# Macaron half steps of a decoder layer: seven products of quarters, with tokens stationary

## The chip, the cores and the metric

The kernel runs on one core of a Trainium2 chip. The metric is the device time of one launch in microseconds (us). Inputs and outputs are fp32; operands of most products are split in two parts of the type fp32r, and three products of parts (high by high, high by low, low by high) stand for one fp32 product.

## The reference

One layer, 512 tokens, model width 1024, hidden width 2816:

```python
h = h + 0.5 * swiglu(rms_norm(h, g_ffn1), w_ffn1_gu, w_ffn1_down)
h = h + hybrid_mixer(rms_norm(h, g_mix), w_in, b_gate, conv_w, w_conv_out, w_attn_out, w_o)
h = h + memory_cross_attention(rms_norm(h, g_cross), rms_norm(mem, g_mem), w_cq, w_ckv, w_co)
h = h + 0.5 * swiglu(rms_norm(h, g_ffn2), w_ffn2_gu, w_ffn2_down)
out = rms_norm(h, g_final)

def swiglu(x, w_gu, w_down):
    gate, up = jnp.split(x @ w_gu, 2, axis=-1)
    return (jax.nn.silu(gate) * up) @ w_down
```

`rms_norm` divides each token by its root mean square and multiplies by a gain per channel. The mixer (a gated convolution and stick-breaking attention of 8 heads) and the cross attention (4 heads over 256 memory tokens) keep their products.

## The kernel before

Activations lie with channels on the partitions and 512 tokens along the rows: h is eight tiles of 128x512. All products outside attention and the value projections are tiles `W^T x`: a block of 128x128 of the weights is stationary and 512 tokens stream past it. `mm3` (L147) issues the three matmuls of a pair of parts.

The work is a list of steps in TensorE's order (`prog`, L154). `run` (L159) goes through the list; weights are loaded by SP two blocks ahead (`load`, 1 MB each into `raw`) and split two steps ahead (`prepare`: ACT copies the high part, DVE subtracts it from the source for the low part, 128x1024 each). Each engine executes its instructions in the order in which the program writes them.

A macaron half step is `ffn` (L324). Up: for 22 chunks of the hidden width a gate tile and an up tile, 24 matmuls of 512 columns each; evacuated on DVE (times 1 / rms, times silu of the gate from ACT) and split into two parts that stay in SBUF. Down: eight output tiles, each 66 matmuls over the 22 chunks, in pairs; `after_ffn1` (L412) adds half of a tile to h as soon as it is summed, splits h for the next stage and squares it for the next norm, while TensorE sums the next tile. `lead` (L378) starts the first two tiles chunk by chunk as x comes in; the norm's factor is applied at evacuation, and evacuations wait (`held`) until it is there. `finish` (L784) does the last two tiles of the second half step by halves of the tokens, so that the first half's norm and output (L814, partly on POOL) run beside the second half's products.

1 / rms (`Norm`): ACT squares, DVE adds, TensorE sums over partitions (`reduce`), DVE does twelve short steps on columns, and a diagonal times a matrix of ones spreads the factor along the rows.

## Time and profile before

| | |
|---|---|
| median of 3 runs | 1440.4 us (1439.62 to 1440.59) |
| span of the profiled execution | 1438.3 us (its own time outside the span is not listed; the median lies 2.1 us above the span) |
| TensorE busy, mean granted clock | 1420.2 us (99%), 0.994 |
| VectorE (DVE), ScalarE (ACT), GpSimd (POOL) busy | 730.0, 543.8, 8.6 us |
| read from and written to memory (HBM) | 135.31 MB, 2.10 MB |

Busy times are of one execution. Matmuls are pipelined: one of 512 columns is listed with 390 ns, and what it costs is the distance from one start to the next. Idle time of an engine costs something only where TensorE, which is busy throughout, waits for it.

### The profile page before, as it was taken

Reading aid. Unit: us, or ns where it says so; the run is one execution under the profiler, and the core shown is the slowest. Engines: PE = TensorE matmul, PEld = TensorE weight load, DVE = VectorE, ACT = ScalarE, POOL = GpSimd, SP = SyncE. Lnnn points to the kernel's source line nnn. Section 1 sums busy time; section 2 is a strip of 40 time slices with the busy share of each in tenths; the row PEclk is TensorE's granted clock in tenths of the full one; section 3 lists DMA queues with packets and bytes.
Section 4 is the critical chain, followed back from the end, with each engine's and each line's share of the span. In section 5 each row is a group of like instructions: output and inputs, shape, how many; then the busy total and the mean of one; then the engine's idle time right before and its main releaser. Section 6 shows DMA issues by size and latency. Waiting matters only on the chain.

```text
span 1438.3 us, 15958 instructions
## 1 busy us (share of the span) xinstructions
PE 1420.2 (99%) x6644; PEld 1193.5 (83%) x6644; DVE 730.0 (51%) x1073; ACT 543.8 (38%) x714; POOL 8.6 (1%) x20
## 2 busy tenths in 40 slices
PE   8999999999999999999999999999999999999996
PEld 7888888888888888888888888988888888888885
DVE  7544444333566664676544447655564544443324
ACT  5323232222365554566332225454442332322222
POOL 0000000000000000000000000000000000000001
PEclk9999999999999999999999999999999999999998
DMA  6223223232312222122223223422223222323221
GB/s 206 88 91 114 88 88 110 81 110 84 114 59 88 85 91 88 62 86 88 88 88 117 89 88 135 147 100 80 97 88 106 99 88 95 111 85 100 88 81 59
DMA packets 23288, 138.43 MB, mean 96 GB/s; under 512 B 2480, under 2 KB 5808, under 8 KB 8880
## 3 DMA queue, kind: packets, MB, share of 16 engines
q1 hardware_dynamic: 23216, 137.42, 28.0%
q8 instruction: 52, 0.85, 0.2%
q14 instruction: 20, 0.16, 0.0%
HBM read 135.31 MB, written 2.10 MB: 96 GB/s over the span
## 4 chain that ended last, share of the span: by engine, by line
PE 98%; DVE 1%; DMA 0%; issue 0%; ACT 0%; SPq 0%; DVEq 0%
PE ps L148 30%; PE ps L150 30%; PE ps L149 30%; PE ps L244 2%; PE ps L246 2%; PE ps L245 2%; PE z L509 1%; PE z L149 1%; PE z L150 1%; PE z L148 1%; DMA h<-in_xt 0%; PE z L277 0%; PE ps L725 0%; PE z L312 0%; DVE a L814 0%
## 5 line engine op out<-in xcount | busy, mean ns | idle before, releaser
L148 PE MATMUL ps<-a,whi 128*128 128x512 f32 (+1 forms) x1878 | 717.9, 382 | 3.0 <-ACT whi L112 3.0
L150 PE MATMUL ps<-a,wlo 128*128 128x512 f32 (+1 forms) x1878 | 717.7, 382 | 0.0
L149 PE MATMUL ps<-a,whi 128*128 128x512 f32 (+1 forms) x1878 | 717.4, 382 | 0.0
L112 ACT ACTIVATE whi<-raw 128x1024 fp32r<-128x1024 f32 (+2 forms) x270 | 269.5, 1002 | 744.6 <-PE ps L149 472.3
L118 DVE TENSOR_TENSOR wlo<-raw,whi 128x1024 fp32r<-128x1024 f32 (+2 forms) x270 | 309.9, 1151 | 212.3 <-ACT whi L112 211.3
L148 PEld LDWEIGHTS ps<-a,whi 128*128 128x128 f32 x1878 | 353.8, 188 | 71.0 <-ACT whi L112 3.7
L149 PEld LDWEIGHTS ps<-a,whi 128*128 128x128 f32 x1878 | 353.7, 188 | 68.1 <-DVE a L120 0.2
L150 PEld LDWEIGHTS ps<-a,wlo 128*128 128x128 f32 x1878 | 353.7, 188 | 68.0
L108 DVE TENSOR_TENSOR a<-ps,a 128x512 f32<-128x512 f32 (+1 forms) x144 | 96.6, 675 | 260.0 <-PE ps L150 259.6
L112 ACT ACTIVATE a<-a 128x512 fp32r<-128x512 f32 (+2 forms) x99 | 58.0, 586 | 83.1 <-DVE a L108 43.4
L118 DVE TENSOR_TENSOR a<-a,a 128x512 fp32r<-128x512 f32 (+2 forms) x99 | 62.2, 632 | 16.4 <-ACT a L112 12.5
L108 DVE TENSOR_TENSOR a<-a,a 128x512 f32<-128x512 f32 x52 | 36.0, 692 | 4.4
L245 PE MATMUL ps<-wlo,a 128*128 128x512 f32 x96 | 37.4, 390 | 0.0
L244 PE MATMUL ps<-whi,a 128*128 128x512 f32 x96 | 37.4, 390 | 0.0
L246 PE MATMUL ps<-whi,a 128*128 128x512 f32 x96 | 37.4, 390 | 0.0
L118 DVE TENSOR_TENSOR w<-w,w 128x1408 fp32r<-128x1408 f32 x16 | 26.0, 1626 | 20.9 <-ACT w L112 20.9
L477 DVE SCALAR_TENSOR_TENSOR w<-z,w 128x512 f32<-128x512 f32 (+1 forms) x24 | 14.7, 641 | 39.9 <-ACT w L474 35.6
L108 DVE TENSOR_TENSOR a<-a,ps 128x512 f32<-128x512 f32 x16 | 11.0, 688 | 45.6 <-PE ps L150 45.6
L260 ACT ACTIVATE a<-h 128x512 f32<-128x512 f32 (+1 forms) x42 | 24.5, 597 | 9.5 <-DVE h L802 9.5
L330 ACT ACTIVATE a<-a 128x512 f32<-128x512 f32 x44 | 27.1, 616 | 2.1 <-DVE a L108 2.1
L268 DVE TENSOR_TENSOR a<-a,a 128x512 f32<-128x512 f32 (+1 forms) x42 | 26.4, 628 | 0.9 <-ACT a L260 0.5
L120 DVE SCALAR_TENSOR_TENSOR a<-h,cst,a 128x512 fp32r<-128x512 f32 x32 | 23.7, 746 | 5.6 <-ACT a L114 5.6
(118 smaller groups left out, 750.3 us busy)
## 6 DMA issues: line engine op xcount, KB each, us to landing
raw<-in_w_gu SPq DMA_DIRECT2D x43, 1024.0 KB, 4.9
raw<-in_w_dn SPq DMA_DIRECT2D x16, 896.0 KB, 4.6
raw<-in_w_dn SPq DMA_DIRECT2D x8, 1024.0 KB, 5.0
raw<-in_w_qk SPq DMA_DIRECT2D x8, 1024.0 KB, 4.9
raw<-in_w_cx SPq DMA_DIRECT2D x8, 1024.0 KB, 4.9
raw<-in_w_gate SPq DMA_DIRECT2D x8, 1024.0 KB, 4.8
raw<-in_w_mix SPq DMA_DIRECT2D x8, 1024.0 KB, 4.9
raw<-in_w_v SPq DMA_DIRECT2D x4, 1024.0 KB, 4.9
```

The source lines that it names most:

```text
L108: nc.vector.tensor_tensor(out=out_, in0=a, in1=b, op=ALU.mult)
L112: nc.scalar.activation(hi, src, AF.Copy)
L118: nc.vector.tensor_tensor(out=lo, in0=src, in1=hi.bitcast(F32), op=ALU.subtract)
L148: nc.tensor.matmul(ps, wh, xh, start=first, stop=False, **kw)
L149: nc.tensor.matmul(ps, wh, xl, start=False, stop=False, **kw)
L150: nc.tensor.matmul(ps, wl, xh, start=False, stop=last, **kw)
L244: nc.tensor.matmul(ps[t], xh[:, c], hi[:, k, :], start=kk == 0, stop=False)
L245: nc.tensor.matmul(ps[t], xh[:, c], lo[:, k, :], start=False, stop=False)
L246: nc.tensor.matmul(ps[t], xl[:, c], hi[:, k, :], start=False, stop=kk == KC - 1)
L260: nc.scalar.activation(sq, h, AF.Square)
L268: nc.vector.tensor_tensor(out=self.acc, in0=self.acc, in1=sq, op=ALU.add)
L330: nc.scalar.activation(g, g, AF.Silu)
```

## The change

Both half steps are computed as products of 2x2 quarters, seven instead of eight, with 15 sums of quarters (Strassen's scheme in Winograd's form), and the roles of the operands are exchanged: 128 tokens by 128 channels are stationary, and 512 (in the last up block 256) columns of weights stream. Results have tokens on the partitions.

Up: x has quarters by tokens (first and last 256) and by channels (chunks 0 to 3 and 4 to 7). `prepare` makes the seven left operands once, with two sums on DVE and two on POOL. A block of weights has 512 gate and 512 up columns as its two column halves, five such blocks and one with 256 and 256. Its four quarters come in units of 128x1024; of each unit POOL makes four sums (`Weights.make`), and all seven right operands are split by ACT and DVE, in 5 buffers of each part, 3 units ahead. `PRODUCTS` gives the order of the seven: A, B, C name the PSUM banks, of which several products add into one. Evacuation joins the banks: silu(gate) times up.

The hidden tiles are turned by TensorE (`turn`, 8 transposes for two chunks), copied by ACT, their four sums made by POOL, and the seven left operands written to DRAM (`hidden`). Down reads them back per product (`part`), splits them, and adds half of each product to the residual, which now has tokens on the partitions (`ht`, for the first half step loaded a second time from x; for the second half step made by 32 transposes, `turn_back`). After the first half step 32 transposes bring h back to channels on partitions. The last norm's factor is now a column per token, and the gain a row. The stages get pools of their own that reuse each other's memory; all 8 PSUM banks are one pool. `lead` and `finish` go.

```diff
+PRODUCTS = ((1, "A"), (5, "C"), (6, "A"), (2, "B"), (7, "A"), (4, "A"), (3, "C"))
+UNITS_AHEAD, LOADS_AHEAD, WBUFS = 3, 4, 5
...
-    def ffn(xs, r, w_gu, w_dn, evac, lead=None, finish=None):
...
+        NEEDS = {1: (0,), 5: (0, 1), 6: (0, 1, 2), 2: (3,), 7: (1, 2), 4: (3,), 3: (2,)}
+        def make(self, i, u):
+            t = self.t
+            b11, b12, b22 = (t.get((q, u)) for q in range(3))
+            def sum_(out, a, b, op=ALU.subtract):
+                nc.gpsimd.tensor_tensor(out=out, in0=a, in1=b, op=op)
+            if i == 5:
+                t["T1", u] = pools["w"].tile([P, 1024], F32, tag="raw", name=nm("raw"))[:, :self.size[u]]
+                sum_(t["T1", u], b12, b11)
+            elif i == 6:
+                sum_(b12, b22, b12)
+                sum_(b11, b12, b11, ALU.add)
+            elif i == 4:
+                sum_(t[3, u], t[3, u], b11)
+            src = {1: b11, 2: t.get((3, u)), 3: b22, 4: t.get((3, u)), 5: t.get(("T1", u)), 6: b11, 7: b12}[i]
+            hi, lo = (pools["w"].tile([P, 1024], F32R, tag=tag, name=nm(tag), bufs=WBUFS) for tag in ("whi", "wlo"))
+            m = self.size[u]
+            split_hi(hi[:, :m], src)
+            split_lo(lo[:, :m], src, hi[:, :m])
+            return [(hi[:, j:j + self.n], lo[:, j:j + self.n]) for j in range(0, m, self.n)]
...
+            def product(place, i, name, units, t):
+                parts = [x for u in units for x in u.parts]
+                if place in (0, 1, 3):
+                    banks[name, t] = bank((P, w.n))
+                ps = banks[name, t]
+                for k, (bh, bl) in enumerate(parts):
+                    ah, al = side(i, k, t)
+                    first, last = k == 0, k == len(parts) - 1
+                    kw = dict(skip_group_check=place not in (0, 1, 3))
+                    nc.tensor.matmul(ps, ah, bh, start=first and place in (0, 1, 3), stop=False, **kw)
+                    nc.tensor.matmul(ps, ah, bl, start=False, stop=False, **kw)
+                    nc.tensor.matmul(ps, al, bh, start=False, stop=last, **kw)
+                evac(i, t, ps)
...
+            for fn, units in self.steps:
+                if units is not None:
+                    upto = min(place[id(units[-1])] + 1 + UNITS_AHEAD, len(self.units))
+                    while made < upto:
+                        x = self.units[made]
+                        need = max(index[id(x.w), q, x.u] for q in Weights.NEEDS[x.i])
+                        load(need + 1 + LOADS_AHEAD)
+                        x.parts = x.w.make(x.i, x.u)
+                        made += 1
+                fn()
...
+    def up(g, r, w_gu, before):
+        plan, parts, sums = Plan(), {}, {}
+        hidden = [dram.tile([P, 7, n, 256], F32, name=nm("hidden")) for _, n in SEGS]
...
+            def put(i, src):
+                hi, lo = (pools["s"].tile([P, 1024], F32R, tag="side", name=nm("s")) for _ in range(2))
+                nc.scalar.activation(half(hi), src, AF.Copy)
+                nc.vector.tensor_tensor(out=half(lo), in0=src, in1=half(hi).bitcast(F32), op=ALU.subtract)
+                parts[i] = hi, lo
...
+            for k in range(KC):
+                nc.scalar.activation(x[k // 4][:, k % 4, :], h[k], AF.Copy, scale=col(g, k))
+                if k == 3:
+                    put(1, a11)
+            s1 = sum_(nc.vector, a21, a22, ALU.add)
+            put(5, s1)
+            s2 = sum_(nc.vector, s1, a11, ALU.subtract)
+            put(6, s2)
+            put(2, a12)
+            put(7, sum_(nc.gpsimd, a11, a21, ALU.subtract))
+            put(4, a22)
+            put(3, sum_(nc.gpsimd, a12, s2, ALU.subtract))
...
+            def fused(out, ps, t):
+                nc.vector.scalar_tensor_tensor(out=out, in0=ps, scalar=rr(t), in1=out, op0=ALU.mult, op1=ALU.add)
+            def evac(i, t, ps):
+                if i == 1:
+                    a["g", t] = small()
+                    nc.scalar.activation(a["g", t], ps, AF.Copy, scale=rr(t))
+                elif i == 6:
+                    a["u", t] = small()
+                    nc.scalar.activation(a["u", t], ps, AF.Copy, scale=rr(t))
+                elif i == 2:
+                    fused(a["g", t], ps, t)
+                    nc.scalar.activation(a["g", t], a["g", t], AF.Silu)
+                elif i == 7:
+                    a["u", t + 2] = small()
+                    nc.scalar.activation(a["u", t + 2], ps, AF.Copy, scale=rr(t + 2))
+                    fused(a["u", t + 2], a["C", t], t + 2)
+                elif i == 5:
+                    a["C", t] = ps
+                elif i == 4:
+                    a["g", t + 2] = small()
+                    nc.scalar.activation(a["g", t + 2], ps, AF.Silu, scale=rr(t + 2))
+                    mul(a["g", t + 2], a["g", t + 2], a.pop(("u", t + 2)))
+                elif i == 3:
+                    fused(a["u", t], ps, t)
+                    mul(a["g", t], a["g", t], a.pop(("u", t)))
...
+        def turn(a, j, m, place):
+            e = pools["e"].tile([P, 8, 256], F32, tag="E", name=nm("e"))
+            for c, (chunk, order) in enumerate(((j, (2, 3, 0, 1)), (j + m, (0, 1, 2, 3)))):
+                ps = bank()
+                for n, t in enumerate(order):
+                    nc.tensor.transpose(out=ps[:, n * P:(n + 1) * P], in_=a["g", t][:, chunk * P:(chunk + 1) * P],
+                                        identity=ident)
+                nc.scalar.activation(e[:, 2 * c:2 * c + 2, :].rearrange("p k c -> p (k c)"), ps, AF.Copy)
+            a21, a11, a12, a22, s1, s2, s3, s4 = (e[:, q, :] for q in range(8))
+            for out_, x, y, op in ((s1, a21, a22, ALU.add), (s2, s1, a11, ALU.subtract),
+                                   (s3, a11, a21, ALU.subtract), (s4, a12, s2, ALU.subtract)):
+                nc.gpsimd.tensor_tensor(out=out_, in0=x, in1=y, op=op)
+            seg = next(n for n, (p, q) in enumerate(SEGS) if p <= place < p + q)
+            nc.sync.dma_start(out=hidden[seg][:, :, place - SEGS[seg][0], :], in_=e[:, 1:, :])
...
+            if late is not None:
+                for slot, job in zip((2, 4), late):
+                    turns[slot] = job
+            if b == 0:
+                plan.step(prepare)
+                plan.step(before)
+            plan.block(w, side, evac, turns)
+            m = n // P // 2
+            late = [lambda a=a, j=j, m=m, p=place + j: turn(a, j, m, p) for j in range(m)]
+            place += m
...
+            def part(i, s=s, n=n, parts=parts):
+                src = pools["s"].tile([P, n * 256], F32, tag="hid", name=nm("hid"), bufs=3)
+                nc.sync.dma_start(out=src, in_=hidden[s][:, SIDE.index(i)].rearrange("p n c -> p (n c)"))
+                hi, lo = (pools["s"].tile([P, n * 256], F32R, tag=tag, name=nm(tag), bufs=3) for tag in ("shi", "slo"))
+                split_hi(hi, src)
+                split_lo(lo, src, hi)
+                parts[i] = hi, lo
...
+                def add(tok, half, src):
+                    o = ht[:, tok, half * 512:(half + 1) * 512]
+                    nc.vector.scalar_tensor_tensor(out=o, in0=src, scalar=0.5, in1=o, op0=ALU.mult, op1=ALU.add)
...
-    def lead(block, evacs):
...
+    def norm1():
+        for k in range(KC):
+            r1.add(h[k])
+        r1.reduce()
+    with phase(w=14):
+        with phase(s=14, e=3, a=11):
+            load_x()
+            hidden = up(G_FFN1, r1, w_gu1, norm1)
+        with phase(t=1, s=3, a=2):
+            ht = pools["t"].tile([P, S // P, D], F32, name="ht1")
+            nc.sync.dma_start(out=ht, in_=xr.rearrange("t p d -> p t d"))
+            sums = spool.tile([P, 4], F32, name="sums1", bufs=1)
+            def squares(i, t):
+                tok = {3: t, 4: t + 2}.get(i)
+                if tok is not None:
+                    sq = pools["a"].tile([P, D], F32, tag="sq", name=nm("sq"))
+                    nc.scalar.activation(sq, ht[:, tok, :], AF.Square, accum_out=sums[:, tok:tok + 1])
+            down(hidden, ht, w_dn1, w_dt1, lambda: None, squares)
+            rm.newton(sums)
+            turned = {}
+            for m in range(KC):
+                ps = bank()
+                for t in range(4):
+                    nc.tensor.transpose(out=ps[:, t * P:(t + 1) * P], in_=ht[:, t, m * P:(m + 1) * P], identity=ident)
+                nc.scalar.activation(h[m], ps, AF.Copy)
+    mixer_pools = phase(w=3, a=61)
+    mixer_pools.__enter__()
...
-    step(rm.reduce)
...
+    rf.reduce()
+    mixer_pools.__exit__(None, None, None)
...
+            def turn_back():
+                for t in range(4):
+                    for half in range(2):
+                        ps = bank()
+                        for m in range(4):
+                            nc.tensor.transpose(out=ps[:, m * P:(m + 1) * P],
+                                                in_=h[4 * half + m][:, t * P:(t + 1) * P], identity=ident)
+                        nc.scalar.activation(ht[:, t, half * 512:(half + 1) * 512], ps, AF.Copy)
...
+            ro.newton(both)
+            for t in (2, 3, 0, 1):
+                o = pools["a"].tile([P, D], F32, tag="o", name=nm("o"))
+                nc.vector.scalar_tensor_tensor(out=o, in0=ht[:, t, :], scalar=ro.cols[:, t:t + 1], in1=gain,
+                                               op0=ALU.mult, op1=ALU.mult)
+                nc.sync.dma_start(out=out[t], in_=o)
```

Three places show the order. First the start, on TensorE. Before (z is the warm-up's bank, ps an output tile, a the parts of x, whi and wlo those of weights):

```order
L81 MATMUL z_76<-ones 128x128 x8
L148 MATMUL ps_105<-a_118,whi_101 128x512
L148 MATMUL ps_106<-a_118,whi_102 128x512
L149 MATMUL ps_105<-a_119,whi_101 128x512
L150 MATMUL ps_105<-a_118,wlo_103 128x512
L149 MATMUL ps_106<-a_119,whi_102 128x512
```

After (s is a left operand's part, a the sum of the squares):

```order
L106 MATMUL z_72<-ones 128x128 x8
L302 MATMUL z_183<-ones,a_160 128x1 x4
L425 MATMUL ps_256<-whi_222,s_120 128x512
L426 MATMUL ps_256<-wlo_223,s_120 128x512
L427 MATMUL ps_256<-whi_222,s_121 128x512
```

The reduction of the first norm (L302) now stands ahead of the first product. It waits for the last of the sums of squares (L293) on DVE, whose queue after the change reads so up to there (L482 makes left operands of x, L143 splits weights):

```order
L293 TENSOR_TENSOR a_160<-a_160,a_171 128x512
L482 TENSOR_TENSOR s_137<-raw_134,s_136 128x1024
L482 TENSOR_TENSOR s_141<-x_115,s_140 128x1024
L482 TENSOR_TENSOR s_147<-raw_144,s_146 128x1024
L293 TENSOR_TENSOR a_160<-a_160,a_174 128x512
L143 TENSOR_TENSOR wlo_223<-raw_212,whi_222 128x1024
L482 TENSOR_TENSOR s_151<-x_115,s_150 128x1024
L482 TENSOR_TENSOR s_157<-raw_154,s_156 128x1024
L293 TENSOR_TENSOR a_160<-a_160,a_177 128x512
L143 TENSOR_TENSOR wlo_229<-raw_214,whi_228 128x1024
L293 TENSOR_TENSOR a_160<-a_160,a_180 128x512
```

The last sum of squares comes behind the left operands of all seven products and two splits of weights; before, the sums of squares stood after the splits of the first two tiles, which TensorE had been fed with.

Second, the middle of up. DVE before (a_367 is 1 / rms along the rows, a others gate, up and their parts):

```order
L118 TENSOR_TENSOR a_803<-a_799,a_802 128x512
L108 TENSOR_TENSOR a_837<-ps_812,a_367 128x512
L118 TENSOR_TENSOR wlo_841<-raw_736,whi_840 128x1024
L108 TENSOR_TENSOR a_869<-ps_844,a_367 128x512
L108 TENSOR_TENSOR a_869<-a_869,a_837 128x512
L118 TENSOR_TENSOR wlo_879<-raw_806,whi_878 128x1024
L118 TENSOR_TENSOR a_873<-a_869,a_872 128x512
L108 TENSOR_TENSOR a_907<-ps_882,a_367 128x512
```

DVE after, in the third block (wlo are low parts of right operands, L517 evacuates):

```order
L143 TENSOR_TENSOR wlo_901<-raw_808,whi_900 128x1024
L143 TENSOR_TENSOR wlo_951<-raw_844,whi_950 128x1024
L143 TENSOR_TENSOR wlo_955<-raw_578,whi_954 128x1024
L143 TENSOR_TENSOR wlo_987<-raw_628,whi_986 128x1024
L143 TENSOR_TENSOR wlo_992<-raw_808,whi_991 128x1024
L517 SCALAR_TENSOR_TENSOR a_873<-ps_995,ny_210,a_873 128x512
L143 TENSOR_TENSOR wlo_1045<-raw_844,whi_1044 128x1024
L517 SCALAR_TENSOR_TENSOR a_888<-ps_1010,ny_210,a_888 128x512
L143 TENSOR_TENSOR wlo_1049<-raw_766,whi_1048 128x1024
L517 SCALAR_TENSOR_TENSOR a_1064<-ps_904,ny_210,a_1064 128x512
```

On POOL there was nothing between the constants and the output:

```order
L87 AFFINE_SELECT fence<-fence 128x128
L89 AFFINE_SELECT fence<-fence 128x256
L100 AFFINE_SELECT a_2621<-ones 128x128
L814 TENSOR_TENSOR a_10238<-a_10098,a_10188 128x256
L814 TENSOR_TENSOR a_10238<-a_10100,a_10188 128x256
```

POOL after, while the third block runs: turned tiles of the second (e) and sums of the fourth's weights (raw):

```order
L557 TENSOR_TENSOR e_930<-e_930 128x256
L385 TENSOR_TENSOR raw_1130<-raw_898,raw_852 128x1024
L557 TENSOR_TENSOR e_930<-e_930 128x256
L385 TENSOR_TENSOR raw_898<-raw_1086,raw_898 128x1024
L557 TENSOR_TENSOR e_930<-e_930 128x256 x2
L385 TENSOR_TENSOR raw_1166<-raw_948,raw_890 128x1024
L385 TENSOR_TENSOR raw_948<-raw_1122,raw_948 128x1024
L557 TENSOR_TENSOR e_1025<-e_1025 128x256 x4
L385 TENSOR_TENSOR raw_852<-raw_898,raw_852 128x1024
L385 TENSOR_TENSOR raw_890<-raw_948,raw_890 128x1024
L385 TENSOR_TENSOR raw_1128<-raw_1128,raw_852 128x1024
L385 TENSOR_TENSOR raw_1164<-raw_1164,raw_890 128x1024
```

DVE has a low part in nearly every row, and POOL has gained sums of 128x1024 whose results a block's later low parts are made of.

Third, from up to down of the first half step, on SP. Before:

```order
L170 DMA raw_1506<-in_w_gu 128x2048
L170 DMA raw_1576<-in_w_gu 128x2048
L170 DMA raw_1646<-in_w_dn 128x2048
L170 DMA raw_1716<-in_w_dn 128x1792
L170 DMA raw_1786<-in_w_dn 128x1792
```

After (ht is the residual, hid a left operand of down, e the last turned chunks; the store from e_2055 waits for POOL):

```order
L559 DMA hidden_113<-e_1864 896x1x256
L559 DMA hidden_113<-e_1949 896x1x256
L371 DMA raw_2198<-in_w_dn 128x1024
L659 DMA ht_2085<-in_xr 128x4x1024
L559 DMA hidden_113<-e_2055 896x1x256
L371 DMA raw_2206<-in_w_dn 128x1024
L598 DMA hid_2088<-hidden_112 128x1536
L598 DMA hid_2184<-hidden_112 128x1536
L598 DMA hid_2254<-hidden_112 128x1536
```

Before, the next blocks of weights were all that SP had to bring; now the first operand of down (hid_2088) stands behind the store of the last turned chunks.

## Rows read from the trace of the kernel before

**Rows 1.** Page: busy us by engine (share, instructions), and the last chain.

```profile
PE 1420.2 (99%) x6644; PEld 1193.5 (83%) x6644; DVE 730.0 (51%) x1073; ACT 543.8 (38%) x714; POOL 8.6 (1%) x20
...
PE 98%; DVE 1%; DMA 0%; issue 0%; ACT 0%; SPq 0%; DVEq 0%
```

**Rows 2.** Windows: stretch, length, busy us by engine, granted clock, DMA share, GB/s.

```profile
6.00:14.00 8.00, 5.77 (x21) 4.22 (x20) 5.12 (x15) 5.68 (x16) 0.00 (x0) 0.87 1.00 345
...
60.00:230.00 170.00, 170.00 (x752) 140.85 (x751) 78.20 (x94) 51.70 (x63) 0.00 (x0) 1.00 0.29 99
230.00:345.00 115.00, 115.00 (x509) 95.29 (x508) 44.02 (x50) 31.94 (x40) 0.00 (x0) 1.00 0.28 93
```

**Rows 3.** Timeline, TensorE at 256 columns: start us, us, engine, line, out<-in, count, idle.

```profile
1416.59 0.28 PE L150 MATMUL ps<-a,wlo 128*128 128x256 f32 x1
...
1416.71 0.28 PE L148 MATMUL ps<-a,whi 128*128 128x256 f32 x1
```

**Rows 4.** Timeline, TensorE, eight transposes of the cross attention and the next matmul.

```profile
959.49 1.03 PE L725 MATMUL ps<-ident,a 128*128 128x128 f32 x8
960.28 0.36 PE L148 MATMUL z<-a,a 128*128 128x256 f32 x1
```

**Rows 5.** Groups by line and shape: engine, out<-in, count, busy us, mean ns, idle.

```profile
L118 DVE TENSOR_TENSOR wlo<-raw,whi 128x1024 fp32r<-128x1024 f32 x222 | 271.2, 1222 | 121.0 <-ACT whi L112 120.8
...
L112 ACT ACTIVATE whi<-raw 128x1024 fp32r<-128x1024 f32 x222 | 235.2, 1060 | 625.7 <-PE ps L149 379.6 <-issue 191.7 <-PE ps L246 28.3
...
L114 ACT ACTIVATE a<-h,cst 128x512 fp32r<-128x512 f32 x32 | 22.6, 713 | 5.7 <-DMA h<-in_xt 2.5 <-DVE h L632 1.7 <-DMA cst<-in_consts 1.5
...
L112 ACT ACTIVATE a<-ps 128x512 fp32r<-128x512 f32 x27 | 15.4, 591 | 4.8 <-PE ps L150 4.3 <-PE ps L725 0.3
```

**Rows 6.** Timeline, DVE near the end of the first half step.

```profile
365.85 0.69 DVE L413 SCALAR_TENSOR_TENSOR h<-ps,h 128x512 f32<-128x512 f32 x1 [2.67 <-PE ps L150]
366.72 1.23 DVE L118 TENSOR_TENSOR wlo<-raw,whi 128x1024 fp32r<-128x1024 f32 x1 [0.18 <-ACT whi L112]
367.86 0.74 DVE L120 SCALAR_TENSOR_TENSOR a<-h,cst,a 128x512 fp32r<-128x512 f32 x1
368.52 0.69 DVE L268 TENSOR_TENSOR a<-a,a 128x512 f32<-128x512 f32 x1
```

**Rows 7.** Line 814, the output products: shortest, median and longest in ns.

```profile
L814 POOL TENSOR_TENSOR a<-a,a x9: 719/719/963, 1422.7 to 1431.4; 128x256 f32<-128x256 f32 x9
L814 DVE TENSOR_TENSOR a<-a,a x7: 410/412/945, 1431.4 to 1433.9; 128x256 f32<-128x256 f32 x7
```

**Rows 8.** Timeline, the last stretch, POOL and DVE.

```profile
1422.70 5.49 POOL L814 TENSOR_TENSOR a<-a,a 128x256 f32<-128x256 f32 x8 [1072.16 <-ACT a L317]
...
1423.93 0.16 DVE L281 TENSOR_SCALAR nv<-z 128x2 f32<-128x2 f32 x1 [1.15 <-PE z L277]
...
1424.84 0.65 DVE L286 TENSOR_SCALAR ny<-nyi 128x2 int32<-128x2 int32 x1
...
1428.24 0.16 DVE L293 TENSOR_TENSOR nb<-na,nv 128x2 f32<-128x2 f32 x1
```

**Rows 9.** Timeline, the first 16 us.

```profile
2.41 0.59 SPq L388 DMA_DIRECT2D h<-in_xt  x1
...
5.57 0.73 PE L148 MATMUL ps<-a,whi 128*128 128x512 f32 x2 [0.74 <-ACT whi L112]
...
12.77 0.63 PE L148 MATMUL ps<-a,whi 128*128 128x512 f32 x1
13.20 0.63 PE L149 MATMUL ps<-a,whi 128*128 128x512 f32 x1
...
15.33 0.42 PE L148 MATMUL ps<-a,whi 128*128 128x512 f32 x1
```

**Rows 10.** DMA issues: out<-in, queue, count, KB each, median us to landing.

```profile
raw<-in_w_dn SPq DMA_DIRECT2D x16, 896.0 KB, 4.6
...
h<-in_xt SPq DMA_DIRECT2D x3, 512.0 KB, 6.5
```

More of the change, by code (lines that the diff above doesn't have):

```diff
@@ L414, in after_ffn1 @@
+    mixer_pools = phase(w=3, a=61)
+    mixer_pools.__enter__()
+    for m in range(KC):
         xm.append(split(h[m], col(G_MIX, m)))
[L415 to L417 removed]
     row2 = act_tile()
```

383 lines of the change are left out of this document (200 added, 183 removed).

## Prediction

> **What bounds the kernel now.** I read the page first, its busy shares and the chain that ended last: TensorE is busy 99% of the span and the chain is 98% TensorE, while VectorE (DVE) stands at 51%, ScalarE (ACT) at 38% and GpSimd (POOL) at 1% [rows 1]. Then the windows, for whether TensorE runs at its pace: over 170 us of the first half step it has no idle time, at a granted clock of 1.00, and issues 752 matmuls, 0.226 us each; the other FFN stretches agree [rows 2]. Last the timeline, for narrower tiles: 256 columns start 0.12 us apart [rows 3]. So time comes off only with TensorE work, and any work given to the idle engines is free only while it stays ahead of TensorE. The two macaron half steps are 2 x 1584 matmuls.
>
> **TensorE's work.** Up before: 44 tiles x 24 = 1056 x 0.226 = 238.7 us. After: five blocks of 7 products x 24 = 168 matmuls at 512 columns, 190 us, and one of 168 at 256 columns, 20.2 us: 210.1, saving 28.6. Down: 528 x 0.226 = 119.3 becomes 11 pairs x 42 = 462 x 0.226 = 104.4, saving 14.9. Both half steps: -87. Added: 88 transposes of hidden tiles and 32 of h per half step, 240 in all; eight of them hold the next matmul off by 0.79 us [rows 4], so 0.1 each: +24. Net **-63 us** if TensorE is always fed.
>
> **What must feed it.** Per full up block TensorE takes 168 x 0.226 + 16 transposes = 39.6 us. In that time:
> ACT: 14 splits x 1.06, ten evacuations and four copies of about 0.6 [rows 5]: 23 us. Covered.
> DVE: 14 low parts of 128x1024, which start 1.14 us apart when back to back, 4 products from SBUF at 0.66 [rows 6], and 6 evacuations from PSUM at 0.69: 16.0 + 2.6 + 4.1 = 22.7 us. Covered, alone.
> POOL: 8 sums of 128x1024 and 8 of 128x256. The only shape of such a sum in the trace is 128x256: 0.719 us [rows 7].
> The two together are another matter. In the last stretch eight POOL sums run back to back, and DVE instructions on a few columns that otherwise take 0.16 us take 0.65, about one POOL sum each; the one that reads PSUM meanwhile takes 0.16. When both engines work on SBUF at 1431 us, one DVE product takes 0.945 instead of 0.410, and the POOL sum 0.963 instead of 0.719 [rows 7, 8]. So a POOL sum shuts out DVE instructions with SBUF operands for about 0.53 us of its 0.72 and is shut out by them: they take turns. For 128x1024 I scale the 0.53 by four: 2.13 us shut, some 2.3 in all. Bounds for the whole sum: 0.72 + 768 columns at DVE's pace, (1.14 - 0.66) / 512 us each [rows 6], gives 1.44; four narrow sums give 2.88.
> The Trainium skill (GPSIMD Engine Reference, 3.1 Elementwise) gives 4497 ns for a sum of 2048 fp32 columns; half of it, an estimate, is 2.25 us, by which the sum below moves by under 1%.
> In turns, a block costs the pair 16.0 + 2.6 + 8 x 2.13 + 8 x 0.53 = 39.9 us, as much as TensorE; with the PSUM evacuations, when they stand behind blocked instructions in DVE's queue, 44.0. I take the middle, 42: +2.4 on four blocks (the first block's sums fall into the start), some +2 on the narrow one: +12. Down: 38.5 low parts of weights x 1.14, 14 of hidden operands (1536 and 1280 columns, by DVE's pace 1.62 + 1.38, seven times), and POOL's 20 wide and 4 half sums, 46.9: 111.8 against TensorE's 104.4; with 28 PSUM adds of 0.69, 131. Middle 121: +17. Both half steps: **+58**, between +17 (perfect turns) and +158 (a wide sum of 2.88, all in series).
>
> **The places where everything stops.** Before, the windows show none at a boundary: from 230 to 345 us, across up to down, TensorE is busy all 115 us [rows 2].
> Start. Before, the first useful matmul is at 5.6 us, chunk by chunk, and some 10 us of TensorE time are lost by 15.3 us, part of it at half clock: after those first gaps matmuls stand 0.43 apart from 12.8 to 15.3 us [rows 9]. Now the norm's reduction is TensorE's first instruction after the warm-up, so nothing starts before all eight squares are added on DVE. Those adds are interleaved with seven 1.14 us low parts and two sums of x. x (2 MB) should be in by about 9 us (a 512 KB piece took 6.5 in that crowd [rows 10]); ACT's eight scaled copies end near 12.5, and the DVE queue from there to the last add is 13 instructions, about 15 us: 28.5 us. In turns with five POOL sums queued at the same time, near 40. I take 40: +30 (bounds +19, +36).
> Up to down, twice. The first hidden operand is loaded by SP behind the spill of the last hidden tiles. From the last up matmul: two DVE instructions 0.85, eight transposes 0.9, two ACT copies 1.2, four POOL sums 2.8, three SP issues 1.8 (0.59 each [rows 9]), the load of 768 KB 4.2 (896 KB lands in 4.6 [rows 10]), ACT's high part 1.5, semaphores about 1: 14.2 us, and 1.3 at half clock afterwards. In the second half step 32 transposes fit in: 2 x 15.5 - 3 = +28.
> Down to mixer. Before, each h tile was updated while the next was being summed. Now the last add, the transposes, eight ACT copies of 0.59, a split of 0.71 and the weights' split of 1.06 stand in a row, and eight splits pace the first tile: 11 us, 3 of them transposes already counted: +8.
> Cross attention to half step 2. After the last h: square, eight scaled copies (5.7), the first operand's split, and ACT has four more operands ahead of the first weights: 15.5 us; seven DVE low parts in turns with POOL's sums put the first weights' low part at 25: +25 (bounds +15, +31).
> End. Four row products and four stores replace the diagonal, the broadcast and sixteen half rows; add and square 2, twelve steps on columns 2.5, products 4.6, the last store 4.4: 13.5 us after the last matmul instead of the 16 up to the span's end [rows 8]: -2.5.
> Sum: 30 + 28 + 8 + 25 - 2.5 = **+88.5**.
>
> **The sum.** The profiled span is 1438.3 us, the median 2.1 above it; I keep that distance: 1440.4 - 63 + 88.5 + 58 = 1524, called **1525 us**.
>
> **Rivals.**
> A. The turns cost nothing beyond the two engines' own time: POOL alone (24 us) and DVE alone (22.7) fit under 39.6, so blocks run at TensorE's pace and the start and half step 2 fall to their lower bounds: 1440.4 - 63 + (19 + 28 + 8 + 15 - 2.5 = 67.5) = 1445 us. For: DVE is only half busy. Against: the 0.65 us instructions.
> B. Not slower: the handovers overlap. Place: the four boundaries. If POOL's sums keep out of the way there and loads, splits and evacuations of neighbouring stages overlap, they cost 15 + 2 x 11 - 3 + 6 + 12 - 3 = 49 us: 1426 us. It decides where they sum to less than 63 with no stall inside the blocks. Against: the issue order, in which spill, load and reduction stand ahead of the first product.
> C. The clock. After the gaps of the start the granted clock averaged 0.87 between 6 and 14 us and matmuls took twice as long for 2.5 us [rows 2, 9]. If waits inside the blocks bring that back for a fifth of the 628 us of FFN matmuls, at 1.2 instead of 2.4 GHz, that is +125 on top, less some 20 of the waiting that it covers: 1630 us. For: the pair is as loaded as TensorE. Against: only that the forecast's waits come to a microsecond or two in a block of 42. The Trainium skill (TensorE: Matmul & The Clock Gate, HAM oscillation) has a kernel whose every tile waits for its feed and starts cold each time; no stretch of this trace shows that in a steady stage.
>
> **How the numbers follow.** Forecast 0.65 (its own range 1480 to 1590), A 0.15, B 0.08, C 0.12. Half of C and B lie outside 1440 to 1615, with a few parts in a hundred of A and of the forecast's ends, under 0.2 together. What differs by less than 0.2% (2.9 us) cannot be told from no change: of A I count 0.03 there, so faster 0.09, same 0.03, slower 0.88.
>
> **What the profile will show.** Right: wide POOL sums near 2.3 us; low parts on DVE whose mean rises from 1.22 to 1.6 or more, though they compute no more; waits of TensorE for wlo and whi inside the blocks; no matmul of a product before 35 us; gaps of 14 us at up to down and 20 or more before half step 2, each followed by a stretch at half clock. Wrong: DVE's low parts still at 1.22 beside busy POOL (A), gaps under 12 us at the handovers (B), clock below 0.9 inside the blocks (C), or an up block under 40 us with TensorE unbroken.

## The result, and the profile after

The changed kernel takes 1532.2 us (median of four runs, 1529.5 to 1533.7) beside 1440.5 us before: a ratio of 1.0637, 95% interval 1.0622 to 1.0652. Forecast were 1525 us. The profiled execution has a span of 1532.0 us, against 1438.3.

The page of the changed kernel, as in [rows 1]: busy time by engine, and the chain that ended last.

```profile
PE 1382.6 (90%) x6492; PEld 1156.1 (75%) x6492; DVE 1100.1 (72%) x1118; ACT 735.5 (48%) x933; POOL 525.1 (34%) x239
...
PE 64%; DVE 20%; issue 6%; POOL 4%; DMA 3%; ACT 3%; SPq 0%; DVEq 0%; ACTq 0%; POOLq 0%
```

TensorE is busy 38 us less, though it idles 150 us instead of 18. A quarter of the chain has gone to VectorE and GpSimd. Groups by shape of those two engines (count, busy us, mean ns, idle before), which answer to [rows 5, 7]:

```profile
L143 DVE TENSOR_TENSOR wlo<-raw,whi 128x1024 fp32r<-128x1024 f32 x344 | 563.2, 1651 | 148.1 <-ACT whi L137 147.3
L133 DVE TENSOR_TENSOR a<-a,a 128x512 f32<-128x512 f32 x48 | 71.6, 1491 | 1.1 <-ACT a L537 0.5
L517 DVE SCALAR_TENSOR_TENSOR a<-ps,ny,a 128x512 f32<-128x512 f32 x60 | 44.3, 739 | 0.0
...
L385 POOL TENSOR_TENSOR raw<-raw,raw 128x1024 f32<-128x1024 f32 x128 | 387.6, 3035 | 219.1 <-DVE wlo L143 210.5 <-issue 3.6 <-DMA raw<-in_w_dn 3.0
L557 POOL TENSOR_TENSOR e<-e 128x256 f32<-128x256 f32 x88 | 110.1, 1258 | 7.6 <-ACT e L553 4.6
L487 POOL TENSOR_TENSOR raw<-x 128x1024 f32<-128x1024 f32 x2 | 4.7, 2352 | 728.8 <-ACT x L491 728.8
```

The low part that took 1222 ns [rows 5] takes 1651 in the mean. GpSimd's wide sum takes 2352 where nothing of VectorE ran as it began (L487), and 3035 in the mean; its narrow one rises from 719 [rows 7] to 1258. VectorE's evacuation that reads PSUM, L517, takes 739, no more than in e5 below (745), where GpSimd sums nothing. One meeting on the timeline (start, duration), ahead of the narrow block, and a low part of half step 2 that came behind a sum:

```profile
240.13 3.36 POOL L385 TENSOR_TENSOR raw<-raw,raw 128x1024 f32<-128x1024 f32 x1
...
240.02 1.21 DVE L143 TENSOR_TENSOR wlo<-raw,whi 128x1024 fp32r<-128x1024 f32 x1
241.15 2.89 DVE L133 TENSOR_TENSOR a<-a,a 128x512 f32<-128x512 f32 x1
...
1138.59 3.35 DVE L143 TENSOR_TENSOR wlo<-raw,whi 128x1024 fp32r<-128x1024 f32 x1
```

GpSimd's sum starts beside a low part and takes 1 us longer than alone; the product on VectorE behind it, 0.69 us alone (686 ns in e5), takes 2.89 and ends 0.55 us after the sum. So here one waits for the other and then runs at its own pace: a queue, not a slower pace.

What TensorE waited for (us in total, times, longest):

```profile
PE z L302 <- DVE a L293: 37.2, 2, 35.0
PE ps L551 <- DVE a L133: 27.6, 9, 7.1
PE ps L425 <- ACT shi L137: 26.4, 2, 15.6
PE ps L426 <- DVE wlo L143: 18.6, 11, 9.1
PE ps L425 <- ACT whi L137: 12.5, 2, 12.0
```

In order: the start, the transposes (for the products of VectorE as above), up to down, and twice, for the most part, the start of half step 2 (9.1 and 12.0 us at a time). ScalarE, which copies the high parts, also waited for GpSimd's sums themselves:

```profile
ACT whi L137 <- POOL raw L385: 75.2, 21, 7.0
```

Windows by stage (columns as in [rows 2]): the second and third wide block, the wide block ahead of the narrow one, the narrow one, up to down, the down's start and rest, and half step 2 from its first product on.

```profile
83.50:123.40 39.90, 39.90 (x186) 33.21 (x185) 33.07 (x24) 22.80 (x28) 29.96 (x16) 1.00 0.38 128
123.40:163.70 40.30, 40.12 (x185) 33.09 (x184) 34.76 (x26) 22.85 (x28) 31.74 (x14) 1.00 0.40 138
203.60:247.90 44.30, 41.01 (x186) 32.97 (x185) 42.46 (x25) 20.10 (x26) 39.06 (x21) 1.00 0.52 178
247.90:280.30 32.40, 24.59 (x186) 23.88 (x184) 25.64 (x19) 15.19 (x23) 25.83 (x13) 0.89 0.20 70
280.30:304.80 24.50, 2.28 (x9) 1.14 (x7) 8.93 (x7) 3.73 (x4) 10.20 (x9) 0.55 0.76 281
...
304.80:310.20 5.40, 5.38 (x12) 4.00 (x13) 5.26 (x3) 2.97 (x2) 0.00 (x0) 0.50 0.70 237
310.20:418.40 108.20, 104.64 (x452) 85.44 (x451) 95.06 (x76) 52.72 (x54) 42.00 (x16) 0.98 0.39 128
...
1131.70:1149.90 18.20, 8.01 (x17) 5.40 (x18) 18.00 (x7) 3.68 (x5) 16.82 (x6) 0.50 0.19 60
```

The second and third wide block run at TensorE's pace or nearly so; most of what is lost is lost where one stage hands over to the next, and in the downs. Up to down, on SP and ACT:

```profile
286.67 1.04 SPq L659 DMA_DIRECT2D ht<-in_xr  x1
292.37 0.53 SPq L559 DMA_DIRECT2D hidden<-e  x1
292.98 0.70 SPq L371 DMA_DIRECT2D raw<-in_w_dn  x1
293.73 2.69 SPq L598 DMA_DIRECT2D hid<-hidden  x3
...
303.29 1.48 ACT L137 ACTIVATE shi<-hid 128x1536 fp32r<-128x1536 f32 x1 [13.39 <-DMA hid<-hidden]
```

The first hidden operand is read behind the last store and beside the 2 MB of the residual, and is there 9.6 us after its issue.

### The profile page after: what moved, and what is told of

Its sections match the earlier page's. It is cut to its first block, busy times and chain, and to the rows that moved or that the text cites. A ratio compares the mean times of both kernels' runs of the same rounds, so it can differ in the third digit from the quotient of the medians.

```text
span 1532.0 us, 16653 instructions
## 1 busy us (share of the span) xinstructions
PE 1382.6 (90%) x6492; PEld 1156.1 (75%) x6492; DVE 1100.1 (72%) x1118; ACT 735.5 (48%) x933; POOL 525.1 (34%) x239
## 4 chain that ended last, share of the span: by engine, by line
PE 64%; DVE 20%; issue 6%; POOL 4%; DMA 3%; ACT 3%; SPq 0%; DVEq 0%; ACTq 0%; POOLq 0%
PE ps L173 12%; PE ps L175 12%; PE ps L174 12%; DVE wlo L143 10%; PE ps L426 6%; PE ps L425 6%; PE ps L427 6%; POOL raw L385 3%; DVE a L133 2%; DVE slo L143 2%; PE ps L271 1%; PE ps L270 1%; DVE s L482 1%; PE ps L269 1%; DVE a L517 1%
## 5 line engine op out<-in xcount | busy, mean ns | idle before, releaser
L143 DVE TENSOR_TENSOR wlo<-raw,whi 128x1024 fp32r<-128x1024 f32 (+1 forms) x358 | 579.0, 1631 | 151.5 <-ACT whi L137 150.7
L137 ACT ACTIVATE whi<-raw 128x1024 fp32r<-128x1024 f32 (+1 forms) x358 | 369.0, 1040 | 489.0 <-PE ps L174 171.6
L385 POOL TENSOR_TENSOR raw<-raw,raw 128x1024 f32<-128x1024 f32 (+1 forms) x136 | 403.3, 2973 | 223.0 <-DVE wlo L143 214.2
L173 PE MATMUL ps<-a,whi 128*128 128x512 f32 (+1 forms) x832 | 317.8, 382 | 3.6 <-ACT whi L137 3.6
L175 PE MATMUL ps<-a,wlo 128*128 128x512 f32 (+1 forms) x832 | 317.5, 382 | 0.5 <-DVE wlo L143 0.5
L174 PE MATMUL ps<-a,whi 128*128 128x512 f32 (+1 forms) x832 | 317.0, 381 | 0.0
L426 PE MATMUL ps<-wlo,s 128*128 128x512 f32 (+1 forms) x672 | 254.3, 378 | 17.2 <-DVE wlo L143 17.2
L425 PE MATMUL ps<-whi,s 128*128 128x512 f32 (+1 forms) x672 | 255.6, 381 | 13.6 <-ACT whi L137 12.0
L487 POOL TENSOR_TENSOR raw<-x 128x1024 f32<-128x1024 f32 x2 | 4.7, 2352 | 728.8 <-ACT x L491 728.8
L427 PE MATMUL ps<-whi,s 128*128 128x512 f32 (+1 forms) x672 | 252.9, 377 | 0.0
L173 PEld LDWEIGHTS ps<-a,whi 128*128 128x128 f32 x832 | 156.9, 189 | 33.9 <-ACT whi L137 3.9
L175 PEld LDWEIGHTS ps<-a,wlo 128*128 128x128 f32 x832 | 156.7, 188 | 31.3 <-DVE wlo L143 1.0
L174 PEld LDWEIGHTS ps<-a,whi 128*128 128x128 f32 x832 | 156.7, 188 | 30.0
L425 PEld LDWEIGHTS ps<-whi,s 128*128 128x128 f32 x672 | 129.4, 193 | 36.4 <-ACT whi L137 12.1
L427 PEld LDWEIGHTS ps<-whi,s 128*128 128x128 f32 x672 | 129.2, 192 | 22.2
L143 DVE TENSOR_TENSOR slo<-hid,shi 128x1536 fp32r<-128x1536 f32 (+1 forms) x28 | 63.7, 2274 | 31.5 <-ACT shi L137 31.4
```

The costliest lines, as they stand in the source:

```text
L137: nc.scalar.activation(hi, src, AF.Copy)
L143: nc.vector.tensor_tensor(out=lo, in0=src, in1=hi.bitcast(F32), op=ALU.subtract)
L173: nc.tensor.matmul(ps, wh, xh, start=first, stop=False, **kw)
L174: nc.tensor.matmul(ps, wh, xl, start=False, stop=False, **kw)
L175: nc.tensor.matmul(ps, wl, xh, start=False, stop=last, **kw)
L385: nc.gpsimd.tensor_tensor(out=out, in0=a, in1=b, op=op)
```

## The experiments

Each ran three rounds beside the kernel before (1439.9 to 1440.1 us). The table is worked out from the starts and ends of the product matmuls on each timeline: "start" to the first product, "block 0" the length of the first wide block, "wide" the four other wide blocks of each half step (range), "2nd" from the last cross-attention matmul to the end of half step 2's block 0; two numbers are the two half steps.

```
                  time     start  block 0  wide        narrow     gap to down  down          2nd
changed kernel    1532.2   41.6   42.1     40.0-44.4   32.5 30.1  24.5 22.4    113.6 114.1   69.3
e1 up on DVE      1490.0   28.6   42.6     40.0-40.1   31.5 30.9  18.5 16.2    114.0 114.4   62.0
e2 no w. sums     1450.7   32.4   39.8     40.0-40.1   22.0 22.1  15.3 14.1    107.7 106.8   59.1
e3 lazy           1536.6   13.5   71.1     40.0-44.4   31.2 32.5  27.2 22.2    112.5 114.0   71.6
e4 fillers        1532.8   39.9   42.5     40.0-44.4   32.5 31.9  24.4 21.5    113.9 114.4   69.4
e5 all on DVE     1455.7   28.8   42.0     40.0        22.0 22.0  17.0 15.4    107.9 107.7   63.2
e6 e1 + lazy      1480.9   13.1   54.8     40.0-40.1   30.8 31.6  19.3 15.0    113.2 115.1   56.9
e7 early read     1504.7   39.7   44.1     40.0-44.5   22.5 22.5  10.5 15.0    121.0 115.4   69.2
e8 combined       1432.3   13.5   54.8     40.0-40.1   22.0 22.1   4.7  8.6    111.1 107.9   56.9
e9 factor later   1439.5   13.3   62.6     40.0-40.1   22.0 22.0   4.7  8.6    110.7 108.5   54.9
e10 + fillers     1439.1   13.2   62.6     40.0-40.1   22.0 22.0   6.5 10.8    110.5 105.9   56.9
e11 unread sums   1607.0   29.1   48.7     45.4-53.8   35.2 33.6  22.1 22.6    122.7 122.3   69.0
```

**e1.** The sums of up on VectorE; the downs keep GpSimd's.

```
 def make(self, i, u):
+    eng = nc.vector if self.up else nc.gpsimd
...
-        nc.gpsimd.tensor_tensor(out=out, in0=a, in1=b, op=op)
+        eng.tensor_tensor(out=out, in0=a, in1=b, op=op)
```

> In both up products every sum (of weights, of activations, of the turned chunks) is VectorE's; the down products keep GpSimd's sums and so are the control. Theory (the loss is where TensorE stands still): with no GpSimd sum beside them the low parts of up return to 1.22 us; VectorE's own work before the first product is then about 7 adds of 0.68, 10 sums and low parts of 1.21 and the first weights' low parts, so the first product starts at 28 to 31 us in place of 41.6; the narrow blocks come down from 32.4 and 30 us to about 23, block 0 of half step 2 from 69 to about 60; the wide blocks stay at 39.6 to 40.5 us, the downs at 113 to 114. Sum about -35: 1497 us. Rival (the prediction's term: turns cost 2.4 us in each middle wide block): the wide blocks come down by 2 us each and the start hardly moves: about 1508 us. Second rival (VectorE becomes the bound, 34.6 us of work in a 39.6 us block): wide blocks at 42 or more, 1540 us.

Ratio 1.0347 (1.0332 to 1.0363), 7 us under the theory's sum. The start came out as the theory said, the wide blocks too. The narrow blocks missed: 31 us, not 23. GpSimd still works there, on the down's sums, which its queue takes ahead of time, and it holds VectorE's narrow sums (four of 0.42 take 5.89):

```profile
242.90 5.80 POOL L387 TENSOR_TENSOR raw<-raw,raw 128x1024 f32<-128x1024 f32 x2 [1.16 <-DVE wlo L143]
...
243.88 5.89 DVE L559 TENSOR_TENSOR e<-e 128x256 f32<-128x256 f32 x4
```

**e2.** `make` without its `sum_` calls; products 4 to 7 read unsummed quarters. (The sums are four of each unit; the expectation's five is a slip.)

> The five sums of weight quarters are left out everywhere (products 4 to 7 read unsummed quarters, so the values are others); the sums of activations stay. It bounds what the weight sums cost. Theory (turns cost little inside wide blocks and in the downs, whose excess over 104.4 us is mostly half clock): wide blocks 39.6 to 40, downs 110 to 112, narrow blocks 23 to 25, start 30 to 33, half step 2's block 0 about 60; about 1490 us. Rival (the prediction's +17 for each down and +12 for each up): downs at 104.5 to 106, and about 1474 us.

Ratio 1.0076 (1.0060 to 1.0091). The weight sums cost 81 us together, more than either side had said, and without them the change still does not pay: -63 us of TensorE's work stand against 74 that are lost otherwise.

**e3.** The operands made one or two products ahead of their own; the first norm's squares are summed on TensorE, which takes seven sums off VectorE. In short:

```
-    (seven put(...) ahead of product 1)
+    job0: x[0:4], put(1)   job1: x[4:8], put(5), norm, put(6)
+    job2: put(2), put(7)   job3: put(4)   job4: put(3)    # ahead of products 1 to 5
```

> Only product 1's left operand is made ahead of product 1; the others are made one or two products ahead of their own, the norm's factor before the third product, and its squares are summed on TensorE. Theory (the start costs because all seven operands are made before the first product): first product at 12 to 15 us in place of 41.6, in half step 2 about 6 us after the cross block in place of 15.6; block 0 then lasts longer (45 to 50 us against 41.9) since VectorE must still make six operands beside it; start gains 22 to 25, half step 2's start 12 to 15; about 1495 us. Rival (VectorE's and GpSimd's work is only moved into block 0, which waits for it there): block 0 ends at 80 us or later and the time is 1525 to 1532 us.

A miss for the theory. The first product came at 13.5 us, and block 0 ended at 84.6 us, as late as before (83.7):

```profile
13.40:84.50 71.10, 56.41 (x233) 45.94 (x234) 63.06 (x43) 33.59 (x39) 49.01 (x16) 0.83 0.34 118
```

VectorE is busy 63 of 71 us there. What the start costs is VectorE's and GpSimd's work, in this order as in the other.

**e4.** Matmuls that nobody reads, where TensorE stands still.

```
+    for _ in range(n): nc.tensor.matmul(z, ones, fence, start=True, stop=True)
```

> Matmuls that nobody reads are put where TensorE stands still: 5 and 15 (half step 2: 5 and 8) of 128x512 f32 around the last turn of each up, 22 ahead of half step 2's first product. Theory (the excess of the downs and of half step 2's start is half clock that follows the standstill): the granted clock stays at 1.0 there, the first down comes to about 105.5 us, the second to about 108, half step 2's block 0 loses about 8; about 1510 us. Rival (the excess is turns on SBUF): the clock rises but the downs stay at 113 us and the time within 3 us of 1532. Second rival (the fillers themselves run at half clock, 1.7 us each, and delay the products): slower, 1540 to 1550 us.

No gain: 1532.8 us. In the windows, up to down, the down's first 6 us, and half step 2's block 0:

```profile
279.00:302.60 23.60, 18.49 (x49) 8.09 (x47) 8.93 (x7) 2.88 (x4) 10.23 (x9) 1.00 0.76 277
303.40:309.40 6.00, 6.00 (x14) 4.44 (x15) 5.28 (x3) 2.97 (x2) 0.00 (x0) 0.50 0.73 237
...
1138.60:1184.50 45.90, 41.02 (x170) 32.67 (x169) 42.46 (x24) 22.98 (x26) 31.55 (x11) 0.96 0.37 114
```

For half step 2 the clock theory falls: at a mean clock of 0.96 instead of 0.83 its block 0 ends 69.4 us after the cross attention, as at 69.3; the weights' low part came from VectorE 26 us after it in either. In the first down it was not tested: the fillers ended at 300.5 us, the clock fell at 302.6, and the first 14 matmuls, from 303.4 on, ran at half clock all the same. The second down began in a stretch at half clock too.

**e5.** e1, and the downs' sums on VectorE too.

> As e1_up_sums_dve, and the downs' sums of weights on VectorE too, so GpSimd sums nothing. Theory (after the first four runs: the sums cost through turns of GpSimd and VectorE, in e1's narrow blocks by the down's GpSimd sums that are made there ahead of time; in the downs VectorE's own work is then the bound: 35 low parts of 1.14 and 7 of 0.6, 14 of 1.7, 28 evacuations of 0.67 and 24 sums of 0.6 to 1.14 are about 112 us against TensorE's 104.4): narrow blocks from 31 to about 24 us, downs 112 to 115, about 1477 us. Rival (what holds the narrow blocks is VectorE's own work, not the turns): narrow blocks stay at 30 or more and the downs grow past 116: 1490 us or more. Second rival (turns alone hold the downs): downs at 107 as without sums, 1463 us.

Ratio 1.0105 (1.0088 to 1.0122), better than the theory and than its best rival. Page, groups, and windows (narrow block; down's start and rest):

```profile
PE 1367.9 (94%) x6492; PEld 1148.8 (79%) x6492; DVE 1043.2 (72%) x1346; ACT 738.2 (51%) x933; POOL 2.2 (0%) x11
```

```profile
L143 DVE TENSOR_TENSOR wlo<-raw,whi 128x1024 fp32r<-128x1024 f32 x344 | 416.9, 1221 | 133.7 <-ACT whi L137 132.4
L387 DVE TENSOR_TENSOR raw<-raw,raw 128x1024 f32<-128x1024 f32 x128 | 155.4, 1220 | 1.4
```

```profile
230.10:252.10 22.00, 22.00 (x187) 22.00 (x185) 21.95 (x32) 13.23 (x21) 0.00 (x0) 1.00 0.39 132
...
269.10:275.20 6.10, 6.07 (x14) 4.57 (x15) 5.28 (x3) 2.97 (x2) 0.00 (x0) 0.50 0.77 261
275.20:377.00 101.80, 101.80 (x451) 84.28 (x451) 87.39 (x90) 52.74 (x54) 0.29 (x1) 1.00 0.41 134
```

VectorE does all of GpSimd's sums and is busy 57 us less. The low parts are back at 1221 ns. The down waits for nothing: of 107.9 us, 3 are the half clock of its first 14 matmuls, the rest is TensorE's work. My bound of 112 us of VectorE work did not hold: it is busy 92.7 us in that down, with 93 instructions where I had added up 108: some 15, by the difference, are done ahead of its first product.

**e6.** e1 with the operands made late, as in e3.

> e1_up_sums_dve with the left operands made one or two products ahead, as in e3_lazy_left. In e3 block 0 ended no earlier, since it waited for the same work of VectorE and GpSimd. Theory (that work, stretched by turns, is what block 0's end is made of; on VectorE alone there is some 56 us of it up to the end of block 0, with 71 us in e1): block 0 of half step 1 ends at 60 to 64 us, that of half step 2 some 6 to 8 us earlier, about 1473 us. Rival (order of the operands does nothing in either form): 1488 to 1492 us.

Ratio 1.0285 (1.0270 to 1.0300): 9 us less than e1, where e3 had gained nothing, and 8 more than the theory's time. Block 0 ended at 67.9 us (71.2 in e1; 60 to 64 were expected), and in half step 2 5 us earlier. In half step 1 VectorE was also spared the first norm's seven sums of 0.69 us, more than the 3.3 us gained there, so that gain is not told apart from the order. In half step 2 no sums were moved: there the later operands and norm factor were worth 5 us with VectorE free of GpSimd, and nothing in e3 (71.6 for 69.3).

**e7.** The down's first two operands read during the last product of up. In short:

```
+    for i in (1, 5):
+        ahead[i] = two raw tiles;  dma_start(ahead[i], hidden[0][:, SIDE.index(i)])
```

> The changed kernel with one thing moved: the down's first two left operands are read back from DRAM during the last product of up (into two buffers each of the pool of unsplit weights) in place of after the last turn and behind the 2 MB load of the residual. Theory (the standstill between up and down is the read that is queued behind the last store and that load): gaps fall from 24.5 and 22.4 us to 10 to 14, the downs stay at 112 to 115, about 1508 to 1512 us. Rival (the down is bound by VectorE from its first product on, so what starts sooner only waits later): the downs lengthen by what the gaps lose, 1525 us or more.

Ratio 1.0446 (1.0430 to 1.0461). Both were half right: the first gap fell by 14 us and the first down grew by 7.4. The narrow blocks fell to 22.5 us unasked: GpSimd worked 17.6 us in the first of them instead of 25.8, and 53.8 in the down behind it instead of 42.0. The early read takes four buffers of the unsplit weights, so that more than one thing was moved; that this is what put the down's sums off was not tested apart.

```profile
247.60:270.10 22.50, 22.31 (x186) 21.97 (x184) 21.06 (x16) 13.44 (x21) 17.61 (x10) 1.00 0.36 126
270.10:280.60 10.50, 2.28 (x10) 1.16 (x8) 10.50 (x7) 3.26 (x5) 10.19 (x7) 0.63 0.64 225
280.60:401.60 121.00, 111.97 (x464) 90.27 (x465) 102.58 (x81) 55.77 (x58) 53.83 (x23) 0.95 0.46 158
```

**e8.** e5, e6 and e7 together.

> All of it together: every sum on VectorE (e5), left operands made late (e6), the down's first two left operands read early (e7). If the parts add up: 1490 less 13 (e5), 17 (e6) and 20 (e7), about 1440 us, within 10 of it: as long as before. Rival (VectorE is the bound once the standstills are gone, so that the gains overlap): 1455 to 1465 us.

1432.3 us, ratio 0.9946 (0.9931 to 0.9960): shorter than the kernel before, by 8 us. That is 8 us better than expected, but the gains do not add up as they were measured: e5's 34.3 and e6's 9.1 us off e1 and e7's 27.5 us off the changed kernel would have made 1419 us of e1's 1490. Some 13 us overlap; 17.6 of e7's gain lay in the narrow blocks, which e5 shortens too. The chain is TensorE's again:

```profile
PE 92%; DVE 3%; ACT 2%; DMA 1%; issue 1%; DVEq 0%; ACTq 0%; SPq 0%
```

**e9.** e8 with the norm's factor and the evacuation of product 1 moved from job1 to job2.

> e8_combined with one thing moved: the norm's nine small VectorE operations and the evacuation of product 1 come one product later, after the operands of the third product. In e8 VectorE stood idle for 5.4 us there in half step 1 (it waited for TensorE's sums of squares, and the operands were queued behind) and began the first low part of half step 2 some 2.3 us late. Theory (block 0 ends when VectorE has made all its operands, so idle VectorE there is time): block 0 ends 4 to 6 us earlier in half step 1 and 2 to 3 us earlier in half step 2: 1424 to 1427 us. Rival (TensorE's half clock in the first 30 us paces it, not VectorE): 1431 to 1433 us.

A miss on both sides: 1439.5 us, 7 more than e8. In half step 1 product 6 adds into the banks of product 1, and their evacuation, 5 us later than in e8, held TensorE for 6.03 us, the rest following at half clock:

```profile
51.08 0.80 PE L432 MATMUL ps<-whi,s 128*128 128x512 f32 x1 [6.03 <-ACT a L556]
```

Half step 2's block 0 ended 2 us earlier, as expected. But e10, which has the same code up to there, ended it as late as e8 did (56.9 us). Block 0 of half step 2 in e8, e9 and e10:

```profile
1069.50:1120.10 50.60, 44.74 (x169) 35.06 (x170) 46.21 (x44) 31.17 (x36) 0.00 (x0) 0.87 0.35 121
...
1077.10:1125.70 48.60, 43.06 (x169) 33.83 (x170) 45.87 (x44) 31.17 (x36) 0.00 (x0) 0.89 0.37 124
...
1078.00:1128.40 50.40, 44.37 (x169) 34.86 (x170) 46.31 (x44) 31.12 (x36) 0.00 (x0) 0.87 0.36 119
```

In e9's profiled execution TensorE's clock was higher there; the 2 us are not shown to come from what was moved.

**e10.** e9 with fillers between the last turn and the downs.

> e9_factor_later with unread matmuls (128x512 f32) between the last turn and the down: 6 in half step 1, 4 in half step 2, about as long as TensorE stood still there in e8. In e4 the granted clock rose and the time stayed, since VectorE was behind. Theory (here VectorE is ahead in the first down, which took 111.1 us with 10 us at half clock against 107.9 in the second with 3): the first down comes to about 108 us, the sum 2 to 3 us less than e9. Rival (as in e4, VectorE is the bound and the clock returns nothing): within 1 us of e9. Second rival (the fillers push back the first product): 2 to 4 us more than e9.

1439.1 us: no difference from e9. In half step 2 the fillers saved the half clock (down 105.9 us for 108.5) and pushed the first product back by 2.2 us; the first down kept its length, and its first product came 1.8 us later.

**e11.** e5 with as many unread sums on GpSimd as the weights had there.

```
+    for _ in range({5: 1, 6: 2, 4: 1}.get(i, 0)):
+        nc.gpsimd.tensor_tensor(out=unread[:, :m], in0=src, in1=src, op=ALU.add)
```

> e5_all_sums_dve (every sum on VectorE) with as many sums added on GpSimd as the changed kernel had there for the weights (four of each set of seven products), reading the same operands and written to a buffer that nobody reads; unsplit weights have 13 buffers for 14, to make room. Nothing on the way to a product waits for GpSimd. Theory (GpSimd's sums cost by lengthening VectorE's operations through turns on SBUF): low parts go from 1.22 back to a mean of 1.65 us or more, the narrow blocks from 22 to 28 to 33, the downs from 108 to 113 or more, as VectorE now has its own sums too; 1510 to 1545 us. Rival (what cost was the chain, products waiting for GpSimd's sums of 2.35 to 3.2 us before the halves could be made): low parts may lengthen, but the time stays at 1455 to 1465 us.

1607.0 us: 151 more than e5, beyond the theory's range and far from the rival's. No product waits for these sums: once the constants of the start are made, no engine and no load waits for GpSimd. The groups, and a wide block:

```profile
L143 DVE TENSOR_TENSOR wlo<-raw,whi 128x1024 fp32r<-128x1024 f32 x344 | 502.8, 1472 | 103.0 <-ACT whi L137 102.3
L387 DVE TENSOR_TENSOR raw<-raw,raw 128x1024 f32<-128x1024 f32 x128 | 187.3, 1467 | 1.7
L563 DVE TENSOR_TENSOR e<-e 128x256 f32<-128x256 f32 x88 | 64.8, 761 | 1.8 <-ACT e L559 1.6
...
131.20:179.60 48.40, 42.37 (x186) 34.16 (x185) 48.19 (x42) 22.57 (x28) 21.96 (x9) 0.96 0.39 125
```

The low parts rise less than expected, 1.47 us for 1.65; the time rises more, as VectorE now has its sums to do as well and is busy 48.2 of 48.4 us in a wide block. The one buffer less is not told apart from the sums. So the turns cost time with no product behind a GpSimd sum. In the changed kernel ScalarE also waits 75.2 us for such sums; no run divides its 76 us between turns and these waits.

## Why the prediction was right

**TensorE's work, -63.** It held. TensorE's busy time, less half of what ran at 0.50, is 1418.0 us before and 1353.3 in e5: -64.7. Where nothing waits (e5), a wide block takes 40.0 us (39.6 forecast), the narrow one 22.0 (21.8), a down 104.9 without its half clock (104.4).

**The feeding, +58.** The mechanism was right: VectorE and GpSimd take turns, and a low part that meets a wide sum takes 3.35 us for 1.21, 2.14 more, where 2.13 were forecast. The total came out by luck. With all sums on VectorE (e5) the kernel takes 76.5 us less; forecast were 58 inside blocks and downs and, by their lower bounds, 11.5 of the start and 10 of half step 2, 79.5 in all. The places were wrong. Changed kernel against e5:

```
                                   forecast   measured
wide blocks but the last, 3 + 3       14.4        4.4
wide block ahead of the narrow, 1 + 1  4.8        8.0
narrow blocks                          4         18.4
up to down                             0         14.5
downs                                 34         12.1
start with block 0                    11.5       12.9
half step 2 up to its block 0         10          6.1
```

The wide blocks and the downs came out 28.7 us below their forecast, the narrow blocks and up to down 28.9 above it: two errors that cancelled. Of the signs that I had named, the low parts rose to 1651 ns; but an up block under 40 us with TensorE unbroken, named as a sign of being wrong, came too (39.90 us, the second wide block).

In the wide blocks I had 39.9 us of turns, or 44.0 with the evacuations in the queue, and took the middle: the low end was right, VectorE keeping 5.5 us idle in the third block. In the narrow block I counted only its own sums; by the runs, GpSimd's queue also held the turned chunks of the wide block ahead and the down's first weight sums, as e1, e5 and e7 show together. In the down the middle of 111.8 and 131 was too high: I counted instructions in it that are done ahead of its first product, as with the bound in e5. Left open is why of the wide blocks just the one ahead of the narrow lost 4 us: the rows show its products of VectorE behind wide sums, and GpSimd busy for 39.1 us in it (31.7 in the third), with the down's first weight sum among them; no run took those sums away alone.

The Trainium skill (SBUF — State Buffer, Who interferes with whom) has it that a VectorE instruction with two SBUF inputs contends with a GpSimd instruction that reads SBUF, for shared ports that are an exclusive lock, while one with at most one SBUF input, outside the two-port modes, does not. The trace agrees: a low part of 1.21 us takes 3.35, a wide sum of 2.35 us takes 3.36, and L517, with one input in PSUM, stays at 739 ns.

**The standstills, +88.5.** First product at 41.6 us (forecast 40), and 28.6 to 28.8 with VectorE alone (28.5 as its lower bound). Cross attention to half step 2: first product after 15.4 us (15.5), the first matmul that needs the weights' low part at 26 (25). Down to mixer 7.1 and a wait of 3.6 behind the first matmuls (11). End 12.9 (13.5). The step that failed is up to down: 14.2 forecast, 24.5 and 22.4 measured. Of what is over, 10.3 and 8.2 us, 7.5 and 7.0 are gone where VectorE makes all sums (17.0 and 15.4 in e5): turns of the last chunks' sums and products, which I had priced at nothing there, and about 1 us by which GpSimd's four sums are longer than VectorE's (0.72 and 0.42 each). The rest goes with the read of the hidden operand: 9.6 us after its issue in half step 1, where the residual's 2 MB was still on its way for the first 4 of them, and 7.3 in half step 2, where I took 4.2 from [rows 10].

**Half clock.** I allowed 1.3 us after each gap to a down. Half of TensorE's busy time in all stretches listed at 0.50 is 21 us in the changed kernel, 2 before; in its first down 12 matmuls took 5.4 us, 2.7 more than at full clock. It is no sum of its own beside the waits: in e4 half step 2's block 0 ran at 0.96 and ended no earlier.

**The rivals.** A (turns cost nothing) is refuted by the low parts at 1651 ns and by e11; nearest to its case is e5, with no sums on GpSimd: 1455.7 us, where A said 1445. B (handovers overlap) came about only in e8, after they were made to, and with 1432 for B's 1426. C did not occur: the granted clock was 1.00 in the wide blocks behind each block 0 (0.83 in block 0 of half step 2, after its gap).
